# Attention of a prompt: probabilities times values as three products of 64 stationary columns

## The chip, the cores and the metric

The kernel runs on one core of a Trainium2 chip. The metric is the device time of one launch in microseconds, taken as the median of several runs. Of the engines the text speaks of PE (TensorE, with PEld for its weight loads), DVE (VectorE), ACT (ScalarE) and POOL (GpSimd).

## What is computed

The whole kernel is one inference step of a two-layer decoder: a gated DeltaNet layer with its feed-forward part, then a layer of dilated sliding-window attention with its own. The change touches the attention of the prompt (1024 positions), three head groups with a window and a dilation of (128, 1), (512, 4) and (2048, 16), 16 heads of 64 in each group, 4 key/value heads:

```python
def dilated_band_attention(q, win, dil, slope, *, k, v):
    ...
    qr = residues(q).reshape(b, dil, nb, B_BLOCK, nkv, qpk, dh)
    kw = key_windows(k)
    vw = key_windows(v)
    ...
    scores = jnp.einsum('brnqgpd,brnkgd->brngpqk', qr, kw, preferred_element_type=jnp.float32) * (dh ** -0.5) + bias
    scores = jnp.where(valid[:, None, None], scores, -jnp.inf)
    lse = jax.nn.logsumexp(scores, axis=-1)
    probs = jnp.exp(scores - lse[..., None])
    out = jnp.einsum('brngpqk,brnkgd->brnqgpd', probs, vw.astype(jnp.float32))
```

## The kernel before

Matrix products are made of 32-bit numbers split in two: a rounded part in the type that TensorE multiplies at full rate (`F32R`, the names with `hi` or `h`), and the rest, rounded too (`lo` or `l`). A product of two split numbers is usually made as three products (hi x hi, lo x hi, hi x lo) added up in PSUM.

`attn_prompt` goes over 24 units: 4 key/value heads, in each the 3 groups, in each 2 pairs of query heads. A unit has a query projection (`q_proj`: 72 products on L1346, evacuated by ACT and DVE in turn on L1356 and L1357) and an attention (`attend`) over 8 blocks of 128 queries. The projection of unit i + 1 runs beside the attention of unit i. When a key/value head is done, `combine` merges its three groups, beside the second unit of the next head; the last head is merged after the loop.

A block goes through five steps, each a push of a pipeline (`stream`), so that five blocks are under way: `scores` (L1431: four products with the keys' two parts; on DVE bias and row minimum on L1435; on ACT the exponential on L1437), a pause, `flip` (L1450: PE transposes the probabilities of two heads; ACT makes the rounded part `ph` on L1453, DVE the rest `pl` on L1454), a pause, and `outputs`, which the change is in. A block has one or two key blocks of 128 (`span`): 15 key blocks in a unit of the first group, 12 in the second, 8 in the third.

`outputs` before: for each key block the stationary operand is 128 columns wide, the values' rounded part in columns 0 to 63 and their rest in 64 to 127 (`vh[:, kb]`, laid out by `load_kv` on L1382 to L1384). Two products (L1468), with `ph` and with `pl` as the moving operand of 256 columns (2 heads x 128 queries), give all four partial products: PSUM rows 0 to 63 hold (ph + pl) x hi, rows 64 to 127 (ph + pl) x lo. Every second block the bank holds two blocks. ACT then copies rows 64 to 127 to the tile `ot` (L1471), and DVE adds rows 0 to 63 and `ot` into the output tile `og`, once for each of the two heads (L1484). The output tile is in natural order, so the addition's destination is dense in the first group, and has steps of 4 and 16 elements in the other two. There are two PSUM banks for this (tag `o`, L1794), and two each for the projection, the scores and the transposes.

The order of the work has two sources. `merge` (L45) takes turns between generators by the share of work that they report: the projection yields 24 times 1/24 (three products each), the attention 40 times 1/30, so the projection is through when the attention is at three quarters of its 40 pushes, and the last two of the 8 blocks have no projection beside them. Then the framework that builds the program places the instructions of each engine in an order of its own and derives the waits; in the trace the products of one block mostly stand together, but not always. Within an engine the order is fixed, and each instruction waits for its operands and buffers.

```python
        seq = [(k0 + j, x[:, j]) for j in range(nk) for x in parts]
        for j, (kb, x) in enumerate(seq):
            nc.tensor.matmul(po[:, b % 2], vh[:, kb].rearrange("p x d -> p (x d)"), x, start=j == 0, stop=j == len(seq) - 1)
        if b % 2:
            t = bp.tile([64, 2, 2, P], F32, name="ot")
            nc.scalar.activation(t, po[64:], AF.Copy)
```

Other lines that the text names: L1389 and after, transposes of the keys in `load_kv`; L1289, the key/value projection, whose last token tile has 64 tokens, and so 64 stationary columns; L987, products of the DeltaNet layer in plain 32-bit type (`F32`), some of them with 64 stationary columns between the dense products of L764; L1294 and L1645, copies out of PSUM.

Of the kernel before, what the change touches and what calls it, by code (L numbers as in the profile page):

```python
# [13 lines left out]
F32 = mybir.dt.float32  # L14
F32R = mybir.dt.float32r
BF16 = mybir.dt.bfloat16
AF = mybir.ActivationFunctionType
# [5 lines left out]
P = 128  # L23
# [1238 lines left out]
class Attn:  # L1262
# [194 lines left out]
    def outputs(self, i, parts, ap, bp, v, st):  # L1457
        nc = self.nc
        ((kv_, g, pr), qs, (kh, kl, vh), dist, stat), b = i
        k0, nk = self.span(g, b)  # L1460
        if b == 0:
            v["o", kv_, pr, g] = ap.tile([P, SP], F32, tag="og", name="og", bufs=7)
        if b % 2 == 0:
            v["po"] = self.bank("o").rearrange("p (b a q) -> p b a q", b=2, a=2)
        o, po = v["o", kv_, pr, g], v["po"]
        seq = [(k0 + j, x[:, j]) for j in range(nk) for x in parts]
        for j, (kb, x) in enumerate(seq):
            nc.tensor.matmul(po[:, b % 2], vh[:, kb].rearrange("p x d -> p (x d)"), x, start=j == 0, stop=j == len(seq) - 1)  # L1468
        if b % 2:
            t = bp.tile([64, 2, 2, P], F32, name="ot")  # L1470
            nc.scalar.activation(t, po[64:], AF.Copy)  # L1471
            for a in range(2):
                rows = o[64 * a:64 * a + 64]
                if g == 0:
                    dst = rows[:, (b - 1) * P:(b + 1) * P].rearrange("p (b q) -> p b q", b=2)
                elif g == 1:
                    dst = rows.rearrange("p (b q r) -> p r b q", b=2, r=4)[:, b // 2]
                else:
                    dst = rows.rearrange("p (q r) -> p r q", r=16)[:, 2 * (b - 1):2 * (b + 1)]
                x0, x1 = po[:64, :, a], t[:, :, a]  # L1480
                if g == 2:
                    x0, x1 = (x.rearrange("p b (c q) -> p b c q", c=2) for x in (x0, x1))
                    dst = dst.rearrange("p (b c) q -> p b c q", b=2)
                nc.vector.tensor_add(dst, x0, x1)  # L1484
        if b == 7:
            pst = self.bank("tr")
            nc.tensor.transpose(pst[:32, :P], stat.rearrange("p x a b -> p (x a b)"), self.ident)
            row = bp.tile([32, P], F32, name="srow")
            nc.vector.tensor_copy(row, pst[:32, :P])
            for x in range(2):  # L1490
                nc.sync.dma_start(st[kv_, g, 2 * pr:2 * pr + 2, x].rearrange("a (b q) -> a b q", q=P), row[16 * x:16 * x + 16])
# [365 lines left out]
```

## Time and profile before

| | |
|---|---|
| median of 3 runs | 3398.77 us (3397.34 to 3402.65) |
| profiled execution | 3405.86 us |
| its span, first to last instruction | 3404.0 us |
| mean granted clock of TensorE | 0.956 |
| PE busy | 3120.5 us, 92% |
| DVE busy | 2295.2 us, 67% |
| ACT busy | 1559.8 us, 46% |
| POOL busy | 1408.4 us, 41% |

The profile is one execution on the chip. Busy time is the union of an engine's instructions; matmuls are pipelined, so that one is marked longer than it holds up the next. "Idle before" is the time that an engine stood ahead of an instruction, with the instruction that ended the wait behind an arrow. A granted clock of 1.00 is 2.4 GHz, 0.5 is 1.2 GHz. All times of the trace count from the span's start.

### The profile page before, as it was taken

The page shows a single profiled execution, that of the slowest core. Times are in us where ns is not written, and L with a number is a line of the kernel's source. Part 1 is how long each engine was busy: PE and PEld are TensorE (multiplying, and loading weights), DVE is VectorE, ACT ScalarE, POOL GpSimd, SP SyncE. Part 2 cuts the span into 40 slices and gives each one's busy share as a digit, 9 for nine tenths or more (in the row PEclk, how much of TensorE's full clock was granted, in tenths as well). Part 3 has the DMA queues.
Part 4 walks back from the last instruction along what each step waited for, and adds up shares of the span by engine and source line. Part 5 has one row for each costly group of instructions (what it writes and reads, how often), then busy time and mean ns, then how long its engine had stood idle before and what let it go on. Part 6 is the DMA issues. An engine that isn't in the chain of part 4 may idle for free.

```text
span 3404.0 us, 53964 instructions
## 1 busy us (share of the span) xinstructions
PE 3120.5 (92%) x19816; PEld 2841.7 (83%) x19816; DVE 2295.2 (67%) x4757; ACT 1559.8 (46%) x3783; POOL 1408.4 (41%) x1350
## 2 busy tenths in 40 slices
PE   7899999999899999899899899997898999998996
PEld 7888888888799999777688888887586999997774
DVE  5667776624665555688957778787656655556888
ACT  5445544434433333433457676776244333334333
POOL 3333333343454444587631313120123544445877
PEclk9999999999999999999899999998899999999998
DMA  4333333345322221411341111111543222214113
GB/s 135 98 99 98 111 105 98 98 123 184 105 77 77 77 77 64 166 68 61 111 144 44 48 43 53 41 37 35 173 133 102 77 77 77 77 64 163 67 65 111
DMA packets 248837, 311.76 MB, mean 92 GB/s; under 512 B 33058, under 2 KB 204306, under 8 KB 248572
## 3 DMA queue, kind: packets, MB, share of 16 engines
q1 hardware_dynamic: 240572, 276.20, 25.7%
q0 software_dynamic: 7856, 31.56, 2.3%
q8 instruction: 156, 2.56, 0.3%
q14 instruction: 109, 0.89, 0.1%
q10 hardware_dynamic: 144, 0.56, 0.0%
HBM read 227.91 MB, written 80.36 MB: 91 GB/s over the span
## 4 chain that ended last, share of the span: by engine, by line
PE 60%; DVE 16%; POOL 8%; ACT 7%; issue 6%; DMA 4%; SPq 0%; POOLq 0%; DVEq 0%; ACTq 0%
PE mm L355 27%; PE mm L394 6%; PE mm L764 5%; PE mm L567 4%; PE mm L1346 3%; PE B L1054 2%; ACT s L1437 2%; PE mm L1289 1%; DVE yc L811 1%; DVE og L1484 1%; DVE qs L1357 1%; DVE wa L380 1%; PE A L987 1%; DMA vT<-qkv 1%; PE o L1697 1%
## 5 line engine op out<-in xcount | busy, mean ns | idle before, releaser
L394 PE MATMUL mm<-wa,ga 128*128 128x512 f32 x1872 | 476.0, 412 | 62.2 <-DVE wa L380 22.0
L394 PEld LDWEIGHTS mm<-wa,ga 128*128 128x128 f32 x1872 | 367.9, 199 | 164.0 <-DVE wa L380 32.4
L764 PE MATMUL mm<-h_hi,w 128*128 128x352 f32 (+1 forms) x1536 | 444.6, 348 | 10.4 <-ACT xr L801 8.0
L1346 PE MATMUL mm<-h_hi,w 128*128 128x352 f32 (+1 forms) x1152 | 361.9, 348 | 0.1
L764 PEld LDWEIGHTS mm<-h_hi,w 128*128 128x128 f32 x1536 | 282.9, 193 | 22.6 <-ACT xr L801 8.9
L323 POOL TENSOR_TENSOR wide<-wide,v 128x288 f32<-128x288 f32 (+1 forms) x176 | 162.7, 939 | 244.3 <-DVE v L322 244.3
L764 PE MATMUL mm<-h_lo,w 128*128 128x352 f32 (+1 forms) x768 | 259.7, 338 | 0.0
L304 DVE TENSOR_TENSOR s<-w,s 128x512 fp32r<-128x512 f32 x132 | 165.2, 1253 | 128.7 <-ACT s L303 128.5
L303 ACT ACTIVATE s<-t 128x512 fp32r<-128x512 f32 x176 | 111.1, 632 | 287.9 <-PE mm L355 277.5
L294 POOL TENSOR_TENSOR t<-w 128x512 f32<-128x512 f32 x88 | 114.5, 1303 | 298.9 <-issue 138.2
L1346 PEld LDWEIGHTS mm<-h_hi,w 128*128 128x128 f32 x1152 | 216.9, 193 | 2.1 <-DVE qs L1357 0.7
L1437 ACT ACTIVATE s<-s,stat 128x128 f32<-128x128 f32 (+1 forms) x384 | 169.1, 442 | 85.1 <-DVE stat L1435 84.0
L145 POOL TENSOR_TENSOR w<-raw,w 128x1024 fp32r<-128x1024 f32 x38 | 100.6, 2649 | 225.3 <-ACT w L142 128.7
L1346 PE MATMUL mm<-h_lo,w 128*128 128x352 f32 (+1 forms) x576 | 192.5, 334 | 0.0
L567 PE MATMUL mm<-mw_hi,o_hl 128*128 128x512 f32 x544 | 175.6, 400 | 4.0 <-ACT o_hl L555 4.0
L304 DVE TENSOR_TENSOR s<-t,s 128x512 fp32r<-128x512 f32 x176 | 131.6, 749 | 39.7 <-ACT s L303 39.5
L355 PE MATMUL mm<-b0h,s 128*128 128x256 f32 (+1 forms) x704 | 144.6, 293 | 12.3 <-ACT s L303 9.7
L1454 DVE TENSOR_TENSOR pl<-tr,ph 128x256 fp32r<-128x256 f32 (+1 forms) x192 | 104.3, 544 | 71.8 <-ACT ph L1453 70.9
L811 DVE SCALAR_TENSOR_TENSOR yc<-xr,convw,yc 128x1112 f32<-128x1112 f32 x72 | 115.9, 1610 | 54.5 <-ACT yc L809 54.4
L764 PEld LDWEIGHTS mm<-h_lo,w 128*128 128x128 f32 x768 | 149.0, 194 | 1.9 <-issue 0.9
L355 PE MATMUL mm<-b6h,s 128*128 128x256 f32 (+1 forms) x704 | 142.8, 292 | 5.1 <-ACT b6h L190 5.1
L355 PE MATMUL mm<-b1h,s 128*128 128x256 f32 (+1 forms) x704 | 142.9, 291 | 4.9 <-ACT y_mix L570 4.9
(487 smaller groups left out, 9452.4 us busy)
## 6 DMA issues: line engine op xcount, KB each, us to landing
w<-in_ffn_w_in_dram SPq DMA_DIRECT2D x88, 512.0 KB
gd<-wide POOLq DMA_DIRECT2D x22, 1088.0 KB, 5.1
graw<-gd SPq DMA_DIRECT2D x44, 544.0 KB
wraw<-in_ffn_w_out_dram SPq DMA_DIRECT2D x44, 512.0 KB
raw<-in_a_w_in_dram SPq DMA_DIRECT2D x32, 512.0 KB
qkv<-f SPq DMA_DIRECT2D x24, 544.0 KB
xo<-x SPq DMA_DIRECT2D x24, 512.0 KB
raw<-in_b_w_q_dram SPq DMA_DIRECT2D x24, 512.0 KB
```

Of the source, the lines that this page charges most:

```text
L294: op(t, x, y)
L303: nc.scalar.activation(out[j][:, 0], x, AF.Copy)
L304: nc.vector.tensor_sub(out[j][:, 1], x, out[j][:, 0])
L323: nc.gpsimd.tensor_tensor(out, out, v, op=ALU.mult)
L355: nc.tensor.matmul(ps[:, :HC[c][1]], u, v, start=z == 0, stop=z == 11)
L394: nc.tensor.matmul(ps, a, b, start=i == 0, stop=i == len(seq) - 1)
L567: nc.tensor.matmul(ps, a, b[:, k], start=k == 0 and i == 0, stop=k == KD - 1 and i == len(seq) - 1)
L764: nc.tensor.matmul(ps[:, :n], a[:, k, :], b[:, k, n0:n0 + n], start=i_ == 0, stop=i_ == 23)
L811: nc.vector.scalar_tensor_tensor(yc, xr[:, j:j + CW], w(j), yc, op0=ALU.mult, op1=ALU.add)
L1346: nc.tensor.matmul(ps[:, :n], a[:, k, :], b[:, k, n0:n0 + n], start=i == 0, stop=i == 23)
L1437: nc.scalar.activation(s[:, a, :n], s[:, a, :n], AF.Exp, bias=m, scale=-1.0, accum_out=stat[:, 1, a, b:b + 1])
L1454: nc.vector.tensor_sub(pl[:, :nk], pt[:, :nk], ph[:, :nk])
```

## The change

The values' two parts are no longer loaded as one stationary operand of 128 columns, but each as one of 64, and three products instead of two are made for a key block, all into PSUM rows 0 to 63: values' hi x `ph`, hi x `pl`, lo x `ph`. The fourth partial product (lo x `pl`) is left out. Of each pair of blocks ACT then copies the first head from PSUM to the output tile, and DVE the second; the copy to `ot` and the additions are gone.

```diff
         o, po = v["o", kv_, pr, g], v["po"]
-        seq = [(k0 + j, x[:, j]) for j in range(nk) for x in parts]
-        for j, (kb, x) in enumerate(seq):
-            nc.tensor.matmul(po[:, b % 2], vh[:, kb].rearrange("p x d -> p (x d)"), x, start=j == 0, stop=j == len(seq) - 1)
+        ph, pl = parts
+        seq = [(vh[:, k0 + j, u], x[:, j]) for j in range(nk) for u, x in ((0, ph), (0, pl), (1, ph))]
+        for j, (w, x) in enumerate(seq):
+            nc.tensor.matmul(po[:64, b % 2], w, x, start=j == 0, stop=j == len(seq) - 1)
         if b % 2:
-            t = bp.tile([64, 2, 2, P], F32, name="ot")
-            nc.scalar.activation(t, po[64:], AF.Copy)
             for a in range(2):
...
-                x0, x1 = po[:64, :, a], t[:, :, a]
+                x = po[:64, :, a]
                 if g == 2:
-                    x0, x1 = (x.rearrange("p b (c q) -> p b c q", c=2) for x in (x0, x1))
+                    x = x.rearrange("p b (c q) -> p b c q", c=2)
                     dst = dst.rearrange("p (b c) q -> p b c q", b=2)
-                nc.vector.tensor_add(dst, x0, x1)
+                if a:
+                    nc.vector.tensor_copy(dst, x)
+                else:
+                    nc.scalar.activation(dst, x, AF.Copy)
```

## Rows read from the trace of the kernel before

**Rows 1.** The page: busy us, share of the span, instructions.

```profile
PE 3120.5 (92%) x19816; PEld 2841.7 (83%) x19816; DVE 2295.2 (67%) x4757; ACT 1559.8 (46%) x3783; POOL 1408.4 (41%) x1350
```

**Rows 2.** Windows: width, busy PE, PEld, DVE, ACT, POOL (instructions), clock, DMA share, GB/s.

```profile
1816.00:2345.00 529.00, 481.82 (x3212) 452.72 (x3211) 418.54 (x1236) 384.37 (x1090) 113.36 (x72) 0.97 0.15 40
```

**Rows 3.** Groups by line and shape, 1760 to 2372 us: busy us, mean ns, idle before.

```profile
L1484 DVE TENSOR_TENSOR og<-o,ot 64x256 f32<-64x256 f32 x192 | 104.0, 541 | 12.5 <-ACT ot L1471 9.5
...
L1468 PE MATMUL o<-ph,vh 128*128 128x256 f32 x280 | 82.8, 306 | 5.1 <-ACT ph L1453 2.9 <-DVE og L1484 1.8
...
L1471 ACT ACTIVATE ot<-o 64x512 f32<-64x512 f32 x96 | 57.1, 595 | 15.4 <-PE o L1468 13.2
```

**Rows 4.** Timeline of PE: start, duration, line, operation, operands.

```profile
2175.44 0.28 PE L1468 MATMUL o<-ph,vh 128*128 128x256 f32 x1
...
2175.91 0.33 PE L1346 MATMUL mm<-h_hi,w 128*128 128x352 f32 x1
```

**Rows 5.** The sum over five windows with the projection in them.

```profile
sum 95.80, PE 94.19 PEld 92.68 DVE 72.10 ACT 69.57 POOL 11.64; mean PE 18.84 PEld 18.54 DVE 14.42 ACT 13.91 POOL 2.33
```

**Rows 6.** The other five windows of that head: two of them, and their sum.

```profile
2079.00:2122.00 43.00, 35.99 (x218) 29.84 (x216) 38.36 (x97) 27.35 (x70) 21.33 (x16) 1.00 0.25 70
...
2189.00:2193.30 4.30, 1.78 (x11) 1.21 (x10) 3.75 (x10) 4.23 (x12) 1.75 (x1) 1.00 0.01 2
...
sum 60.30, PE 46.85 PEld 38.97 DVE 53.04 ACT 44.19 POOL 26.28; mean PE 9.37 PEld 7.79 DVE 10.61 ACT 8.84 POOL 5.26
```

**Rows 7.** L1468 alone (PE, PEld) in the five windows of rows 5.

```profile
2059.90:2079.00 19.10, 3.20 (x18) 2.90 (x18) 1.00 0.13 32
2122.00:2140.00 18.00, 3.71 (x23) 3.47 (x24) 1.00 0.01 3
2146.00:2165.00 19.00, 3.03 (x18) 2.85 (x18) 1.00 0.24 67
2170.00:2189.00 19.00, 3.34 (x18) 2.89 (x18) 1.00 0.12 32
2193.30:2214.00 20.70, 2.90 (x14) 2.70 (x14) 0.92 0.25 68
```

**Rows 8.** Timeline of PE at the end of the key/value projection's 64-token tile.

```profile
1720.62 0.39 PE L1289 MATMUL mm<-w,h_hi 128*64 128x512 f32 x1
1720.86 1.04 PE L187 MATMUL sm<-ident,xn 128*128 128x128 f32 x8
```

**Rows 9.** Groups by line: copies from PSUM; last, min/median/max of the additions.

```profile
L1645 DVE COPY kt<-tr 128x264 f32<-128x264 f32 x8 | 3.4, 427 | 0.6 <-PE tr L1640 0.6
...
L1356 ACT ACTIVATE qs<-mm 64x288 fp32r<-64x288 f32 x48 | 27.9, 582 | 3.1 <-PE mm L1346 2.5 <-DVE qs L1357 0.6
L1294 ACT ACTIVATE kv_o<-mm 64x256 f32<-64x256 f32 x3 | 0.9, 371 | 2.4 <-PE mm L1289 2.4
...
L1484 DVE TENSOR_TENSOR og<-o,ot x192: 401/599/631, 1778.7 to 2370.2; 64x256 f32<-64x256 f32 x192
```

**Rows 10.** Who waited for whom: total us, times, longest.

```profile
ACT qs L1356 <- DVE qs L1357: 14.5, 29, 1.1
```

**Rows 11.** Timeline of DVE, then of PE, at a unit's end.

```profile
2190.85 1.19 DVE L1484 TENSOR_TENSOR og<-o,ot 64x256 f32<-64x256 f32 x2
...
2192.73 0.30 PE L1431 MATMUL sc<-kh,qs 128*128 128x128 f32 x1 [1.64 <-DVE stat L1435]
```

**Rows 12.** L1484 alone in the windows of rows 6: the long one, and the sum.

```profile
2079.00:2122.00 43.00, 4.13 (x10) 1.00 0.25 70
...
sum 60.30, DVE 8.97; mean DVE 1.79
```

**Rows 13.** Timeline of PE in the recurrent layer.

```profile
107.41 0.32 PE L764 MATMUL mm<-h_lo,w 128*128 128x352 f32 x1
107.57 0.32 PE L764 MATMUL mm<-h_hi,w 128*128 128x352 f32 x1
107.81 0.33 PE L987 MATMUL A<-kT 128*64 128x64 f32 x2
```

## The prediction

> **What bounds the kernel now.** I read the profile's page first: TensorE is marked busy 92% of the span, weight loads 83% [rows 1]. The profiled execution took 3405.86 us, 1.9 us more than its span of 3404.0 and 7.1 us (0.2%) more than the 3398.77 us median of the three runs; I work out a difference on the trace and put it on the median. 0.2% of the median, 6.8 us, is also about what a measurement of this kernel can tell from no change.
>
> The change sits in the prompt's attention, some 610 us from 1760 us on. A table by stretch shows what kind of stage that is: in 529 us of it TensorE is marked busy 482 us, VectorE 419 us, ScalarE 384 us, at a granted clock of 0.97 [rows 2]. The reader is to see three engines near their limits, so shares don't decide and the stage has to be cut finer.
>
> The groups by line give the pieces: two times 280 products of 256 columns on L1468 (the row with `pl` is the twin of the one with `ph`), 96 copies `ot` on ScalarE of 595 ns, and 192 additions `og` on VectorE of 541 ns, 104.0 us in all [rows 3]. The 0.3 us that a product is marked there overlaps with its neighbours; what it takes from the stream is the distance of starts. In a timeline of four products in a row, the first starts at 2175.44 and the next line's product at 2175.91: 0.47 us for four, so **0.12 us each** [rows 4].
>
> I then cut one key/value head (2059.9 to 2216.0 us, the third of four) into ten windows. Five of them, 95.8 us together, are those in which the query projection is interleaved: TensorE is marked busy 94.2 us of them, VectorE only 72.1, ScalarE 69.6 [rows 5]. There TensorE sets the time. The other five, 60.3 us, are the ends of units, where there is no projection left to put between, and a long one in which the previous head is merged: TensorE 46.9, VectorE 53.0, ScalarE 44.2 [rows 6]. In those, VectorE or ScalarE sets the time: in the one at 2189 us TensorE has 1.78 of 4.3 us, ScalarE 4.23.
>
> **What is added: 280 products.** A key block has two products now and three after, so 560 become 840. At 0.12 us, 280 x 0.12 = 33.6 us of TensorE's stream. In the TensorE-bound windows stand 18 + 23 + 18 + 18 + 14 = 91 of this head's 140 products [rows 7], 65%. I take the same share of the whole: 0.65 x 33.6 = **21.8 us exposed**. The other 11.8 us fall where TensorE idles 13.4 us per head (60.3 less 46.9 [rows 6]); I count them at nothing, the cover being VectorE's and ScalarE's queues. If that cover goes, the 11.8 come back, and 33.6 is the upper bound.
>
> A product with 64 stationary columns and 256 moving ones doesn't occur. Below: the same 0.12 us, since it moves the same 256 columns. The nearest rows are the key/value projection's last token tile, also of the rounded 32-bit type by the code (L162, L1289): 64 stationary columns, 512 moving: the last starts at 1720.62, the transposes after it at 1720.86 [rows 8], so 0.24 us for twice the columns, and next to nothing extra on leaving. I take 0.12. The upper bound is the rival of the mode, below.
>
> **What is removed and moved: the copy out.** Per pair of blocks, one `ot` copy (64x512) and two additions go; one ScalarE copy and one VectorE copy, each 64x256, come.
> - VectorE. The nearest copy out of PSUM is 128x264 in 427 ns with a dense output [rows 9]; the additions of 64x256 run from 401 (dense output) to 631 ns (spread), 599 in the middle [rows 9]. A dense addition thus costs what a copy does, and I price the copy like the addition, 541 ns. 96 of 192 go: **-52 us of VectorE's work**. Bounds: 427 gives -63, 631 gives -43.
> - ScalarE. A dense 64x256 copy out of PSUM is 371 ns (three of them). With an output spread by 1, 4 and 16 elements in turn, 64x288 takes 582 ns on average [rows 9]; if the dense third is near 390 (371 for 256 columns, and 32 more), the spread two thirds are near 680. So the new copy is some 380 ns for the undilated third, some 620 for the rest: 32 x 380 + 64 x 620 = 52 us against 96 x 595 = 57. **-5 us**, and in two of three groups ScalarE gets no shorter. Bounds: 371 for all, -21 us; 680 for all, +8.
> - Does VectorE's copy still wait for ScalarE's? It needs no result of it now. But ScalarE's second `qs` copy waits 29 times, 14.5 us, for VectorE's operation on the first, with which it shares only the bank in PSUM [rows 10]. So I expect the two copies of a bank to go one after the other, as now (`og` waited 9.5 us for `ot` [rows 3]). Bounds: 0 and -9.5 us of VectorE idling.
> - ScalarE's copy waits for the block's last product, as `ot` did; behind it in that queue are the exponentials of the next blocks. That product is up to 0.24 us later. No DMA is added or moved; the spare tile `ot` only frees memory.
>
> **What the saving is worth.** VectorE's 52 us count only where it is waited for. At 2189 us this can be seen: TensorE stands 1.64 us until VectorE's `stat`, and shortly before that VectorE ran two `og` of 1.19 us together [rows 11]. One of them goes. In the five windows outside TensorE's, `og` takes 9.0 us of VectorE per head, of it 4.1 in the long one [rows 12]. There VectorE has 38.4 of 43 us and ScalarE 27.4 [rows 6]: the half of 4.1 counts in full, 2.1 us, three times (after the last head it is merged elsewhere): 6.2. In the four short ones ScalarE is as full as VectorE or fuller (4.23 against 3.75 us of 4.3), so of the half of 4.9 I count half, 1.2 us, four times: 4.8. **Together -11 us**; bounds 0 and -18 (4 x 4.5).
>
> **Sum:** +21.8 - 11.0 = +10.8 us. 3398.8 + 11 gives **3410 us**.
>
> **Rivals.**
> 1. The two cancel (no change). If half of the exposed 21.8 us is swallowed at the next unit end, where TensorE waits anyway, 10.9 - 11.0 is nothing: 3399 us. For: each unit has such a wait. Against: VectorE's 72.1 of 95.8 us [rows 5] says that it carries no backlog into it, so the end starts later too.
> 2. Faster: the unit ends are set by work that doesn't hang on the added products (`qs` and key splits already queued), so all of the 21.8 is absorbed, and VectorE's saving counts in full: -18, 3381 us. It decides from the point where more than half of the exposed time is absorbed. For: `og` stands shortly before the awaited `stat` [rows 11]. Against: ScalarE, which hardly gets shorter, is full there.
> 3. Entering and leaving 64 columns costs a drain. In the recurrent layer four products of 64 columns stand between products of 128: the step in is 0.24 us (107.57 to 107.81) where the same product otherwise takes 0.16 (107.41 to 107.57) [rows 13]: 0.08 us, and I take as much for the step out. With at least 192 visits (24 units of 8 blocks) of 0.16 us that is 31 us more: 3410 + 31 = 3441 us. Against: those are plain 32-bit products by the code, and the rounded ones of rows 8 leave without a pause.
>
> The Trainium skill, "TensorEngine Tiling (Array Packing)", section "Key Properties", states that changing the tiling mode drains TensorE, which speaks against this change; by that rule the time is rival 3's. This trace agrees for the plain type and not for the rounded one (0.24 us on leaving), and I go by the latter.
>
> **Chances.** Forecast (over 3406, its own range 3406 to 3425) 0.45; rival 1 0.29; rival 2 0.18; rival 3 0.08. So faster 0.18, same 0.29, slower 0.45 + 0.08 = 0.53. The range reaches down into rival 2, whose lower half it leaves out (0.09), and up to the full 33.6 us less a little relief, 3430, without rival 3 (0.08): 3388 to 3430.
>
> **What would show it.** Right: 840 products on L1469 or so, still 0.12 us apart, no pause around them; windows with the projection longer by some 0.06 us per old product, TensorE as full as before; VectorE's group of copies near 52 us; shorter waits for `stat` and `pl` at unit ends. Wrong: the projection windows unchanged in length (rival 1 or 2); a gap of weight loads before the first or after the last 64-column product (rival 3); ScalarE's copies well over 620 ns, which would turn the unit ends longer; or a changed order of instructions that opens waits in the projection windows.

## The result and the profile after

The changed kernel took 3383.25 us (median of 7 runs, 3378.46 to 3390.45), the kernel before, beside it on the same chip, 3401.23 us (7 runs, 3393.71 to 3406.94). The ratio is **0.9948, interval 0.9932 to 0.9963**: 18 us faster, with an interval of 13 to 23 us. The forecast was 11 us slower, and the range's lower end was 3388 us: forecast and range were both wrong.

The busy line of the page after, which answers to [rows 1]:

```profile
PE 3121.5 (92%) x20096; PEld 2847.5 (84%) x20096; DVE 2252.6 (67%) x4661; ACT 1541.1 (46%) x3783; POOL 1408.5 (42%) x1350
```

TensorE has 280 instructions more and is marked busy 1 us longer; VectorE lost 43 us, ScalarE 19. The groups by line of 1754 to 2360 us, as in [rows 3] (the products and the two copies):

```profile
L1469 PE MATMUL o<-ph,vh 128*64 128x256 f32 x560 | 135.3, 290 | 0.3
...
L1469 PE MATMUL o<-pl,vh 128*64 128x256 f32 x280 | 79.9, 286 | 0.0
...
L1486 ACT ACTIVATE og<-o 64x256 f32<-64x256 f32 x96 | 51.9, 541 | 0.8 <-PE o L1469 0.7
L1484 DVE COPY og<-o 64x256 f32<-64x256 f32 x96 | 51.7, 539 | 9.4 <-ACT og L1486 8.0
```

There are 840 products. (Behind L1468 the changed kernel's lines stand up to two further on.) VectorE's copy takes 539 ns and ScalarE's 541, and VectorE waits 8.0 us for ScalarE's copy of the same bank. A timeline of TensorE, which answers to [rows 4]:

```profile
2176.85 0.32 PE L1346 MATMUL mm<-h_hi,w 128*128 128x352 f32 x1
2177.01 0.28 PE L1469 MATMUL o<-ph,vh 128*64 128x256 f32 x1
2177.13 0.28 PE L1469 MATMUL o<-pl,vh 128*64 128x256 f32 x1
2177.24 0.28 PE L1469 MATMUL o<-ph,vh 128*64 128x256 f32 x1
2177.36 0.32 PE L1346 MATMUL mm<-h_hi,w 128*128 128x352 f32 x1
```

The 64-column products start 0.12 us apart, and nothing is added on entering (0.16 us, the distance that projection products have among themselves) or on leaving (0.12 us).

**Where the time went.** I cut both profiled executions at the first and the last score product (L1431) and at the decode's first product of cache keys. A window from the first to the last score product, before and then after (width, busy time of PE, PEld, DVE, ACT, POOL, granted clock, DMA share, GB/s):

```profile
1759.90:2362.50 602.60, 547.53 (x3668) 516.62 (x3668) 475.89 (x1420) 443.27 (x1264) 125.46 (x78) 0.97 0.15 41
```

```profile
1754.80:2349.30 594.50, 560.08 (x3943) 531.63 (x3943) 432.33 (x1335) 425.97 (x1265) 123.75 (x78) 0.99 0.17 47
```

The attention became 8.1 us shorter with 275 more of TensorE's instructions on record in it. TensorE's time without a mark fell from 55.1 (602.6 - 547.5) to 34.4 us. The granted clock rose from 0.97 to 0.99: the window before has 34.1 us at the lower of the two levels, the window after 13.7, each such stretch behind a pause of TensorE. A part of one of them in the kernel before, and two products in it:

```profile
2195.00:2198.00 3.00, 3.00 (x13) 3.00 (x12) 1.53 (x7) 1.47 (x7) 0.00 (x0) 0.50 0.68 191
```

```profile
2195.41 0.52 PE L1346 MATMUL mm<-h_lo,w 128*128 128x384 f32 x1
2195.73 0.52 PE L1346 MATMUL mm<-h_hi,w 128*128 128x384 f32 x1
```

Products of 384 columns start 0.32 us apart there, and 0.17 us at the upper level (2198.40 and 2198.57). So the clock gives at most half of the 20.4 us, some 10 us, and that is as much as the whole shortening. The decode's first product of cache keys, before and then after (duration min/median/max, first and last start):

```profile
L1660 PE MATMUL s<-kt,qb x160: 279/386/690, 2385.3 to 2472.4; 128*64 128x256 f32 x64, 128*64 128x264 f32 x64, 128*64 128x136 f32 x32
```

```profile
L1662 PE MATMUL s<-kt,qb x160: 279/386/690, 2358.7 to 2443.6; 128*64 128x256 f32 x64, 128*64 128x264 f32 x64, 128*64 128x136 f32 x32
```

From the last score product to it passed 22.8 us before (2385.3 - 2362.5) and 9.4 us after (2358.7 - 2349.3): 13.4 us less. I call this stretch **the gap**. The rest is the start of the attention, 5.1 us earlier with the same instructions ahead of it, so by how much two executions differ, and the part behind the gap, 0.7 us longer: -8.1 - 13.4 - 5.1 + 0.7 = -25.9, the difference of the spans (3404.0 and 3378.1). Half of it thus lies in a stretch of which the prediction doesn't speak. The queue of SP shows what happens there, before and then after (start, time, line, DMA):

```profile
2360.43 1.21 SPq L1491 DMA_DIRECT2D st<-srow  x2
...
2369.25 1.21 SPq L1491 DMA_DIRECT2D st<-srow  x2
2371.83 1.25 SPq L1575 DMA_DIRECT2D kc<-in_cache_k_dram  x2
```

```profile
2332.26 1.27 SPq L1577 DMA_DIRECT2D kc<-in_cache_k_dram  x2
...
2345.61 1.28 SPq L1493 DMA_DIRECT2D st<-srow  x2
...
2357.48 1.27 SPq L1493 DMA_DIRECT2D st<-srow  x2
```

The decode's first cache load, `kc`, was the last in line before, behind the row writes of the last units. After the change it goes ahead of the last two of them, 17 us ahead of the last score product.

### The profile page after: what moved, and what is told of

Its sections match the earlier page's. It is cut to its first block, busy times and chain, and to the rows that moved or that the text cites. A ratio compares the mean times of both kernels' runs of the same rounds, so it can differ in the third digit from the quotient of the medians.

```text
span 3378.1 us, 54405 instructions
## 1 busy us (share of the span) xinstructions
PE 3121.5 (92%) x20096; PEld 2847.5 (84%) x20096; DVE 2252.6 (67%) x4661; ACT 1541.1 (46%) x3783; POOL 1408.5 (42%) x1350
## 3 DMA queue, kind: packets, MB, share of 16 engines
q1 hardware_dynamic: 240572, 276.20, 25.9%
## 4 chain that ended last, share of the span: by engine, by line
PE 63%; DVE 14%; POOL 8%; ACT 6%; issue 6%; DMA 3%; SPq 0%; POOLq 0%; ACTq 0%; DVEq 0%
PE mm L355 27%; PE mm L394 6%; PE mm L764 5%; PE mm L1346 5%; PE mm L567 4%; PE B L1054 2%; PE mm L1289 1%; DVE yc L811 1%; ACT s L1437 1%; PE sc L1431 1%; PE o L1469 1%; DVE wa L380 1%; PE A L987 1%; PE tr L1450 1%; DVE qs L1357 1%
## 5 line engine op out<-in xcount | busy, mean ns | idle before, releaser
L394 PEld LDWEIGHTS mm<-wa,ga 128*128 128x128 f32 x1872 | 364.5, 197 | 167.2 <-DVE wa L380 34.1
L764 PE MATMUL mm<-h_hi,w 128*128 128x352 f32 (+1 forms) x1536 | 440.4, 345 | 10.3 <-ACT xr L801 8.1
L1346 PE MATMUL mm<-h_hi,w 128*128 128x352 f32 (+1 forms) x1152 | 354.4, 342 | 0.0
L764 PEld LDWEIGHTS mm<-h_hi,w 128*128 128x128 f32 x1536 | 280.1, 191 | 22.1 <-ACT xr L801 9.0
L1346 PEld LDWEIGHTS mm<-h_hi,w 128*128 128x128 f32 x1152 | 212.3, 189 | 1.6
L1346 PE MATMUL mm<-h_lo,w 128*128 128x352 f32 (+1 forms) x576 | 189.3, 329 | 0.0
```

The source lines that it names most:

```text
L394: nc.tensor.matmul(ps, a, b, start=i == 0, stop=i == len(seq) - 1)
L764: nc.tensor.matmul(ps[:, :n], a[:, k, :], b[:, k, n0:n0 + n], start=i_ == 0, stop=i_ == 23)
L1346: nc.tensor.matmul(ps[:, :n], a[:, k, :], b[:, k, n0:n0 + n], start=i == 0, stop=i == 23)
```

## The experiments

Ratios are to the kernel before, run beside each kernel on the same chip; 0.001 is 3.4 us.

**Parts of the change, with the loads held in place.** In all kernels said to be pinned, the decode's cache loads are kept behind the last row write on SP, where they stood before:

```diff
-                nc.sync.dma_start(st[kv_, g, 2 * pr:2 * pr + 2, x].rearrange("a (b q) -> a b q", q=P), row[16 * x:16 * x + 16])
+                self.last_st = nc.sync.dma_start(st[kv_, g, 2 * pr:2 * pr + 2, x].rearrange("a (b q) -> a b q", q=P), row[16 * x:16 * x + 16])
...
+            with tc.issue_after(self.last_st.ins):
```

The kernel before with the pin alone:

> The kernel before, with the decode part's cache loads tied on SP's queue behind the last write of the softmax rows (st), where the kernel before has them anyway. Every theory: as the kernel before, within 0.2%, decode's first score product about 23 us after the attention's last one. It is the base for the three runs beside it.

The changed kernel with the pin:

> The changed kernel with the same tie of the cache loads. Theory A (the 18 us come from two places: about 8 from the attention itself and about 12 from cache loads that stand earlier on SP's queue): 12 us slower than the changed kernel, so some 8 us (0.2%) faster than the kernel before, with the gap between the attention's last score product and decode's first one back at 20 us or more. Theory B (all of it comes from the attention, the loads' place is worth nothing): as the changed kernel, 18 us (0.5%) faster than the kernel before.

The products alone (old copy-out):

```diff
-        seq = [(k0 + j, x[:, j]) for j in range(nk) for x in parts]
+        seq = [(k0 + j, x[:, j]) for j in range(nk) for x in (*parts, parts[0])]
```

> The kernel before with the tie, and a third product of 128 columns for each key block (ph a second time, so that the sum is another one); the copy out is the old one. 280 products of 0.12 us alone. By the prediction's exposed share: +22 us on p0 (bounds 12 to 34). By the absorbed view (rival 2): under +5 us.

The copy-out alone (the two old products):

```diff
-            t = bp.tile([64, 2, 2, P], F32, name="ot")
-            nc.scalar.activation(t, po[64:], AF.Copy)
...
-                nc.vector.tensor_add(dst, x0, x1)
+                if a:
+                    nc.vector.tensor_copy(dst, x)
+                else:
+                    nc.scalar.activation(dst, x, AF.Copy)
```

> The kernel before with the tie, its two products of 128 columns, and the new copy out: ScalarE copies the first head, VectorE the second, rows 64 to 127 (values' rest) are left out. The copy's saving alone. By the prediction: -11 us on p0 (bounds 0 to -18). If the saving was mis-sized and the exposed share was right: -30 us or more. If the products were absorbed and the saving right: -8 to -18.

And twice as many products as before, with the old copy-out:

> The kernel before with four products per key block instead of two, 128 stationary columns each (the sum holds the first probabilities three times), copy-out as before; cache loads pinned behind the last row write. 67 us more of TensorE's stream, at 0.12 us each. p2_third_product, with 33.6 us more, was 1.5 to 4.5 us slower only. Theory K (stalls of TensorE in the attention take the first 30 or so us and little more): +20 to +40 us, ratio 1.006 to 1.012. Rival (VectorE and ScalarE set the pace throughout, TensorE has room for all of it): +3 to +10 us, ratio 1.001 to 1.003.

Measured: pin alone 1.0003 (0.9988 to 1.0019); changed and pinned 0.9961 (0.9948 to 0.9974); third product alone 1.0013 (1.0001 to 1.0025); copy-out alone **0.9919** (0.9899 to 0.9939); four products 1.0058 (1.0046 to 1.0070). The window from the first to the last score product, in the order pin alone, third product, fourth product, copy-out alone, changed and pinned:

```profile
1753.50:2352.80 599.30, 544.14 (x3668) 513.05 (x3668) 475.83 (x1420) 442.64 (x1264) 125.63 (x78) 0.98 0.15 41
```

```profile
1758.10:2364.20 606.10, 565.41 (x3943) 538.11 (x3944) 477.81 (x1421) 444.61 (x1265) 123.37 (x78) 0.99 0.15 41
```

```profile
1758.30:2378.10 619.80, 590.72 (x4218) 571.05 (x4219) 477.88 (x1419) 446.08 (x1265) 126.73 (x78) 0.99 0.15 40
```

```profile
1757.30:2333.90 576.60, 536.11 (x3667) 508.19 (x3667) 436.33 (x1332) 422.68 (x1265) 123.33 (x78) 0.99 0.17 45
```

```profile
1754.90:2355.50 600.60, 565.89 (x3943) 537.16 (x3943) 433.15 (x1337) 425.99 (x1265) 123.23 (x78) 0.98 0.16 43
```

Width less PE is TensorE's time without a mark: 55.2, 40.7, 29.1, 40.5 and 34.7 us. With the old copy-out 280 more products add 21.3 us of marked time, and the stretch grows by 6.8 only, since 14.5 us of unmarked time go. In the timings they cost 3 us (1.0013 less 1.0003, at most some 13 by the outer ends, 1.0025 less 0.9988). The next 280 cost 15 (1.0058 less 1.0013): the room was nearly used up. With the new copy-out the first 280 cost 14 us (0.9961 less 0.9919). The copy-out alone saves some 28 us (0.9919 less 1.0003), more than the whole change. The pin also gives most of the gap back: 21.6 us with the pin alone (2374.4 - 2352.8), 17.4 us in the changed and pinned kernel (2372.9 - 2355.5).

The room for the products wasn't in the stretches that TensorE is marked to fill. Two runs of projection products (L1346) in the third head, with the pin alone and then with the third product:

```profile
2146.36:2155.16 8.80, 8.80 (x65) 8.73 (x64) 7.08 (x21) 5.45 (x15) 0.00 (x0) 1.00 0.37 95
2195.47:2203.61 8.14, 8.14 (x59) 8.07 (x59) 5.92 (x22) 5.25 (x19) 0.00 (x0) 1.00 0.38 103
```

```profile
2158.34:2167.49 9.15, 9.15 (x68) 9.07 (x67) 7.20 (x21) 6.37 (x19) 0.00 (x0) 1.00 0.32 90
2206.97:2215.33 8.36, 8.36 (x61) 8.29 (x61) 6.12 (x22) 5.33 (x19) 0.00 (x0) 1.00 0.36 100
```

TensorE is marked busy all the time; three and two products of L1468 are added, and the runs are 0.35 and 0.22 us longer, 0.11 to 0.12 us for each. There the products cost what they were priced at. Here is the whole window, cut into such runs (no break of over 1.1 us between two products of L1346) and the rest, in us:

| | runs | of L1468 in them | rest | TensorE unmarked in the rest | at the lower clock, in both |
|---|---|---|---|---|---|
| pin alone | 440.6 | 353 of 560 | 158.5 | 51.9 | 23.9 |
| third product | 436.0 | 437 of 840 | 169.9 | 33.7 | 10.2 |
| copy-out alone | 439.9 | 356 of 560 | 136.5 | 33.4 | 17.1 |
| changed and pinned | 432.5 | 434 of 840 | 167.9 | 32.3 | 27.3 |

Of the 280 added products only 84 stand in the runs with the old copy-out, and 78 with the new one. The others stand in the rest, where TensorE waits. The third product alone takes those waits from 52 to 34 us, the copy-out alone takes them to 33, and both together leave 32: they draw on the same waits. That is one reason why the products cost 3 us in one kernel and 14 in the other. (The lengths of the runs alone don't show a cost: the framework orders TensorE's other products anew in these kernels, and some 70 of them leave the runs.)

The clock is another. In the kernel before, 0.001 more of an execution's mean granted clock goes with 1.7 to 2.3 us less time (six sets of 16 to 28 executions), and the kernels differ in it by several times that. Means of the executions, against those of the kernel before beside them; the last two columns are an estimate at 2 us for each 0.001:

| kernel | time, us | mean clock | the clock's part | left |
|---|---|---|---|---|
| third product, pinned | +3.9 | +0.0045 | -9 | +13 |
| copy-out alone, pinned | -28.1 | +0.0025 | -5 | -23 |
| changed and pinned | -14.1 | +0.0051 | -10 | -4 |
| changed (second measurement, below) | -18.1 | +0.0056 | -11 | -7 |
| changed, `ot` kept (below) | -11.3 | +0.0055 | -11 | 0 |
| before, one buffer of `ot` (below) | -17.9 | +0.0038 | -8 | -10 |

By this the third product's 3 us are a cost of some 13 us, most of which the clock gives back, and of the changed kernel's 18 us more than half come with the clock. (0.001 of 3400 us is 6.8 us at the other level, so at most 3.4 us of work.) Since the lower stretches stand behind pauses of TensorE, the clock isn't apart from the edits; but no run holds it in place, and how much of each difference is the clock's stays an estimate.

**What the copy-out saves by.** Three theories: the work that goes from the two engines, the order in which they have to read one bank, and how evenly each pair's copies are shared. First both copies on VectorE:

```diff
-                if a:
-                    nc.vector.tensor_copy(dst, x)
-                else:
-                    nc.scalar.activation(dst, x, AF.Copy)
+                nc.vector.tensor_copy(dst, x)
```

> Two products of 128 stationary columns as before, both copies out on VectorE and none on ScalarE; the products' second half (rows 64 to 127 of the bank) isn't added, so the sum lacks the rest of the values; cache loads pinned behind the last row write. Compared with the kernel before, ScalarE loses some 57 us of copies and VectorE keeps its 104 us (192 copies for 192 additions). Theory V (it is VectorE's work that TensorE waits for, and the new copy-out paid by halving it): most of the 28 us of p3_new_copy are lost again, ratio 0.998 to 1.001. Theory C (the chain from the last product of a pair over ScalarE's copy to VectorE's two additions held the bank and both queues; or ScalarE's work counted): ratio 0.991 to 0.995, as p3_new_copy.

Then, by the same edit with the other call, both on ScalarE:

> The same with both copies on ScalarE and none on VectorE. Against the kernel before VectorE loses 104 us, ScalarE gains 2 x 53 - 57 = some 49 us. Theory V: VectorE's relief counts fully, ratio 0.985 to 0.992, at least as fast as p3_new_copy. Theory S (both engines are near their limit, and ScalarE becomes what TensorE waits for): ratio 0.996 to 1.003.

Measured 0.9948 (0.9936 to 0.9961) and 0.9948 (0.9930 to 0.9966): 19 us of the 28 (0.9948 less 1.0003), both times. Neither theory V nor theory S holds; it makes no difference which engine is relieved. Then the old copy-out without the data dependence:

```diff
-                x0, x1 = po[:64, :, a], t[:, :, a]
+                x0, x1 = po[:64, :, a], self.ident[:64, None, :].to_broadcast([64, 2, P])
```

> The kernel before with VectorE's additions reading the identity tile instead of ScalarE's copy ot: the same 96 copies and 192 additions of the same sizes, but an addition no longer needs the copy's result; cache loads pinned behind the last row write. The sum holds a constant in place of the values' second half. Theory C (the chain over the two engines, last product, ScalarE's copy, VectorE's two additions, is what the new copy-out shortened): a good part of the 17 us that both one-engine variants gained, ratio 0.994 to 0.998. Theory W (what counts is work: all three variants with the new copy-out took some 55 us off the two engines together): ratio 0.999 to 1.001.

0.9996 (0.9985 to 1.0007), but it doesn't show what I wanted it to. A timeline of ScalarE and VectorE in it:

```profile
2104.85 0.59 ACT L1471 ACTIVATE ot<-o 64x512 f32<-64x512 f32 x1
...
2105.48 0.42 DVE L1484 TENSOR_TENSOR og<-o,ident 64x256 f32<-64x256 f32 x1 [0.44 <-ACT ot L1471]
```

The addition still waits for a copy whose result it doesn't read. The two share the bank alone. The Trainium skill, "PSUM — Partial Sum Buffer", section "PSUM bank collisions raise a hardware error", says that the compiler's back end orders any two engines that touch one bank in the same 32 partitions, readers too; here one reads rows 64 to 127 and the other rows 0 to 63, and they are ordered all the same (9.6 us in 26 waits). So the bank had to go as well:

```diff
-            nc.scalar.activation(t, po[64:], AF.Copy)
+            nc.scalar.activation(t.rearrange("p b a q -> p (b a) q"), self.ident[:64, None, :].to_broadcast([64, 4, P]), AF.Copy)
```

> As r1_unchained, and ScalarE's copy ot (still 64x512) reads the identity tile instead of the bank in PSUM: the number and sizes of the operations on ScalarE and VectorE stay, but nothing of the copy-out stands between the two engines any more, and VectorE's additions shouldn't show a wait for ot (26 waits, 9.6 us, in r1_unchained although the data were independent). The sum holds a constant in place of the values' second half; cache loads pinned. Theory C (the order of the two engines at one bank is what cost the time): ratio 0.994 to 0.997. Theory W (it is the work of some 55 us that the new copy-out takes off): ratio 0.999 to 1.001.

0.9993 (0.9979 to 1.0006). This doesn't tell the two apart either, for another reason: copies that wait for nothing were all issued early. The group of `ot`, then the windows of the first key/value head and of the other three:

```profile
L1471 ACT ACTIVATE ot<-ident x96: 612/620/656, 1744.7 to 1877.7; 64x512 f32<-64x512 f32 x96
```

```profile
1755.00:1904.60 149.60, 135.22 (x916) 128.80 (x916) 108.53 (x329) 137.26 (x375) 21.04 (x11) 0.97 0.17 45
1904.60:2355.10 450.50, 412.64 (x2752) 385.61 (x2753) 363.22 (x1091) 287.73 (x885) 102.25 (x68) 0.98 0.14 39
```

And the same two windows of the kernel with both copies on VectorE:

```profile
1754.80:1893.70 138.90, 131.23 (x917) 127.00 (x917) 106.67 (x329) 96.65 (x289) 21.51 (x11) 0.99 0.18 49
1893.70:2342.10 448.40, 410.40 (x2752) 383.10 (x2752) 362.62 (x1091) 287.63 (x885) 102.26 (x68) 0.98 0.15 43
```

With `ot` crowded into the first head, that head is 10.7 us longer at 40.6 us more of ScalarE's work, with no order at a bank at all (at most 3 of the 10.7 are the clock's: 10.2 us at the lower level against 3.4); in the other three, where both kernels have the same work, they take nearly the same. So ScalarE's work seems to cost time even where TensorE is marked busy 135 of 150 us; TensorE's order of work is another in this kernel, too, and the two aren't parted. How much of the 19 us the order at the bank adds stays open.

**Sharing.** Both copies of a bank on one engine, in turn from pair to pair: the same work as in the change on each engine, and no order at the bank.

```diff
-                if a:
+                if b // 2 % 2:
                     nc.vector.tensor_copy(dst, x)
```

In the changed kernel, not pinned:

> The changed kernel with both copies of a bank on one engine, ScalarE and VectorE in turn from pair to pair: as much work for each engine as in the changed kernel, and none of its 19 waits (8.0 us) of VectorE's copy for ScalarE's at the same bank. Theory C: 4 to 10 us faster than the changed kernel, ratio to the kernel before 0.990 to 0.993. Theory W, or TensorE setting the pace: as the changed kernel, 0.994 to 0.996.

With the two old products, pinned:

> The two products of 128 stationary columns, both copies of a bank on one engine, ScalarE and VectorE in turn from pair to pair (p3_new_copy with the copies shared out as in s2_engine_by_pair); the sum lacks the rest of the values; cache loads pinned. Theory E (work taken off the two engines counts by a third, 55 us for 17; sharing each pair evenly between them is worth another 11 us; the added products then cost some 14): a saving like that of the two one-engine variants, ratio 0.993 to 0.997. Rival (turn by turn is bad in itself, through the order of work that it makes): ratio 0.998 to 1.002.

Both copies on VectorE, three products, pinned:

> The changed kernel with both copies on VectorE; cache loads pinned. By theory E the saving of 17 us of q1_two_copies_vector less some 14 for the products: ratio 0.997 to 1.001. Rival (the products cost nothing where the copy-out is uneven, as with the old copy-out): ratio 0.994 to 0.996.

And the changed kernel, not pinned, with the engines exchanged (`if not a` for `if a`):

> The changed kernel with the two copies exchanged: VectorE takes the first head, ScalarE the second. The same work on each engine, shared evenly in each pair. By theory E as the changed kernel, ratio 0.993 to 0.996. Rival (the gain hangs on the particular order of work that the changed kernel has): anywhere up to 1.000.

All of the copy-outs together:

| copy-out of a pair | two products | three products |
|---|---|---|
| before's: copy `ot`, two additions | 1.0003 (0.9988 to 1.0019) | 1.0013 (1.0001 to 1.0025) |
| one copy on each engine | 0.9919 (0.9899 to 0.9939) | 0.9961 (0.9948 to 0.9974) |
| both on VectorE | 0.9948 (0.9936 to 0.9961) | 1.0010 (0.9999 to 1.0022) |
| both on ScalarE | 0.9948 (0.9930 to 0.9966) | not run |
| both on one engine, in turn | 0.9946 (0.9928 to 0.9963) | 0.9999 (0.9988 to 1.0010), not pinned |

Every way to copy without the addition takes 58 to 65 us off the two engines together (by the windows, against the pin alone) and saves some 19 us with two products. Sharing each pair evenly saves 9 to 10 more (0.9948 or 0.9946 to 0.9919) and 17 with three (1.0010 to 0.9961). Theory C fell here as the main cause: the variants without order at a bank are the slower ones. In each new copy-out that was run both ways the third product costs 14 to 21 us. With the engines exchanged: **0.9916** (0.9896 to 0.9936), median 3379.37 us, at least as fast as the changed kernel with the same three products; the interval overlaps that of the changed kernel's second measurement, below, by a little. So the gain doesn't hang on one lucky order. TensorE's other products stand in another order in each variant of the copy-out, though, and what that does isn't parted from the sharing.

Why sharing counts is argued, not shown. Of the waits, those of VectorE and of ScalarE that lead the lists, before and then after (total us, times, longest):

```profile
DVE pl L1454 <- ACT ph L1453: 70.9, 74, 1.4
...
ACT s L1437 <- DVE stat L1435: 84.0, 95, 1.8
```

```profile
DVE pl L1454 <- ACT ph L1453: 105.7, 99, 2.0
...
ACT s L1437 <- DVE stat L1435: 90.0, 101, 1.6
```

In many blocks VectorE waits for ScalarE's `ph` and ScalarE for VectorE's `stat`. So the two queues may largely work one after the other, and two copies in a row on one of them (1.1 us) may hold up both. One wait fits this for sharing in turn: with two products, VectorE waits 41.5 us (60 times) for ScalarE's `qs` copies, and 11.6 us (32 times) with one copy on each engine. With both copies on VectorE it is 10.0 us (32 times), so this isn't the whole cause.

**Work that no longer counts.** The values' split moved to GpSimd:

```diff
-        nc.scalar.activation(vh[:, :, 0], t[:, :, 2], AF.Copy)
-        nc.vector.tensor_sub(vh[:, :, 1], t[:, :, 2], vh[:, :, 0])
+        nc.gpsimd.tensor_copy(vh[:, :, 0], t[:, :, 2])
+        nc.gpsimd.tensor_sub(vh[:, :, 1], t[:, :, 2], vh[:, :, 0])
```

> The changed kernel with the splitting of the values (12 copies of 628 ns on ScalarE, 12 subtractions of 693 ns on VectorE) moved to GpSimd, which is busy 122 of 585 us in this stage: VectorE -8.3 us, ScalarE -7.5 us. If work of ScalarE and VectorE still counts by about half, as in the experiments so far: 3 to 8 us faster than the changed kernel, ratio to the kernel before 0.991 to 0.994. If TensorE alone sets the pace now: as the changed kernel, 0.995.

> The changed kernel itself, beside the other two: ratio 0.993 to 0.997, as measured before.

0.9943 (0.9928 to 0.9957) against 0.9942 (0.9928 to 0.9957): nothing. 16 us of work taken off once per group, ahead of need, are worth nothing.

**The place of the cache loads.** A first try in the kernel before, not pinned:

```diff
-                nc.sync.dma_start(st[
+                (nc.gpsimd if kv_ == NKV - 1 and g == 2 else nc.sync).dma_start(st[
```

> The kernel before, unpinned, with the row writes of the last key/value head's last group issued on GpSimd's queue instead of SP's, so that the decode's cache loads no longer stand behind them on SP. Theory A (the place of the cache loads on SP is worth the 12 us by which the gap between the last score product and the decode's first product shrank in the changed kernel's trace): ratio 0.996 to 0.998. Rival (the gap is filled by the last head's merging anyway, or the loads are waited for elsewhere): ratio 0.999 to 1.001.

1.0002 (0.9989 to 1.0015). The loads hardly moved, though the row writes of the last two units no longer stood ahead of them:

```profile
2359.71 0.67 SPq L1514 DMA_DIRECT2D mst<-st  x2
2368.45 1.28 SPq L1575 DMA_DIRECT2D kc<-in_cache_k_dram  x2
```

SP issues nothing for 8 us and then the load. So the row writes weren't what held it, and theory A wasn't tested by this. What the change also does is to give back `ot`, two buffers of 2 KB per partition, which later tiles can take. Two kernels part this from the rest: the changed one with `ot` kept,

```diff
+            t = bp.tile([64, 2, 2, P], F32, name="ot")
+            nc.gpsimd.memset(t[:, 0, 0, :8], 0.0)
```

> The changed kernel with the tile ot allocated as before (two buffers of 64x512) and touched once per pair by a GpSimd write of eight columns, which nothing reads. Theory M (the memory that ot gives back lets the decode's cache tiles start earlier: in the changed kernel's trace kc is issued at 2332.26 us, ahead of the last two row writes, and before behind them): kc is issued behind the last row write again, the gap between the last score product and the decode's first is 15 to 22 us instead of 9, and of the gain some 4 to 6 us are lost: ratio 0.996 to 0.998. Rival (the place of the loads has another reason, or is worth nothing): as the changed kernel, 0.994 to 0.995.

and the kernel before with half of it given back:

```diff
-            t = bp.tile([64, 2, 2, P], F32, name="ot")
+            t = bp.tile([64, 2, 2, P], F32, name="ot", bufs=1)
```

> The kernel before, unpinned, with one buffer for ot instead of two, nothing else. Theory M: the cache loads are issued early as in the changed kernel, the gap between the last score product and the decode's first shrinks from 22 to 8 to 12 us, and the time falls by 4 to 13 us, ratio 0.996 to 0.999 (a second copy ot then waits for the additions of the first, which stand a pair earlier: nothing). Rival: 0.999 to 1.001.

With `ot` kept 0.9967 (0.9956 to 0.9977); **with one buffer less, and nothing else changed, 0.9946 (0.9926 to 0.9966)**, as much as the whole change. SP's queue with `ot` kept (its lines stand four further on than before), then with one buffer:

```profile
2349.44 1.21 SPq L1495 DMA_DIRECT2D st<-srow  x2
2351.99 1.26 SPq L1579 DMA_DIRECT2D kc<-in_cache_k_dram  x2
```

```profile
2345.29 1.27 SPq L1575 DMA_DIRECT2D kc<-in_cache_k_dram  x2
...
2359.27 1.28 SPq L1491 DMA_DIRECT2D st<-srow  x2
...
2367.16 1.31 SPq L1491 DMA_DIRECT2D st<-srow  x2
```

Kept, the load is behind the last row write again; freed, it is ahead of the last two. In the kernel with one buffer the attention and the decode's first product:

```profile
1756.40:2361.30 604.90, 551.39 (x3668) 520.47 (x3668) 475.38 (x1421) 443.53 (x1264) 124.96 (x78) 0.96 0.16 45
```

```profile
L1660 PE MATMUL s<-kt,qb x160: 279/386/689, 2371.7 to 2455.9; 128*64 128x256 f32 x64, 128*64 128x264 f32 x64, 128*64 128x136 f32 x32
```

The gap is 10.4 us (2371.7 - 2361.3) against 22.8 before, and the attention is no shorter (604.9 against 602.6). TensorE's and ScalarE's instructions in the attention stand in the same order as before. Theory M holds, and more than I expected of it: the trace shows 12 us, the timing 18 (12 to 25).

## Why the prediction was wrong, point by point

- **"Together -11 us; bounds 0 and -18"** is the step that failed by most: the copy-out alone is worth some 28 us, or some 23 without what is put down to the clock. The prices were right (VectorE's group went from 104.0 [rows 3] to 51.7 us, ScalarE's from 57.1 to 51.9), and the copies of one bank do go one after the other. It also counts where I looked for it: between the pin alone and the copy-out alone the runs of projection products stay as long (440.6 and 439.9 us), and the rest goes from 158.5 to 136.5. Wrong was how much it counts there: I took half of the time of `og` in those windows, with 18 us as the bound, and the rest became 22 us shorter in the traces. Why it gains more than VectorE's own time isn't shown.
- **"the spare tile `ot` only frees memory"** put at nothing what lay in the next stage. Freed memory is what let the cache loads start early: the gap is 9.4 us in the changed kernel, and 17.4 and 21.8 with the loads held back (pinned, and `ot` kept, 2365.6 - 2343.8). It is worth 18 us in the timing alone, and 4 to 6 us on top of the rest. I looked for DMAs that the change adds or moves and found none in its lines; the one that it moved belongs to the next stage.
- **The clock had no term**, though [rows 7] show 0.92 in one window behind a unit's end, where TensorE had waited. It is put at nothing without a reason, and by the estimate above it goes with 10 to 11 us of the changed kernel's gain.
- **"0.65 x 33.6 = 21.8 us exposed"** came out about right in size (14 to 21 us with the new copy-outs) and not in its way. The share was taken from the old products, of which 63% stand in the runs (353 of 560); of the added ones 30% do (84 of 280). That the others count "at nothing" holds only as long as TensorE waits in the rest anyway. The prediction names this ("If that cover goes, the 11.8 come back") but not that its own saving takes the cover: 3 us for the products and 28 for the copy-out make 14 together, not 25. "There TensorE sets the time" stands where I could look: in two runs that are marked full each product cost its 0.11 to 0.12 us.
- The sum: with the loads pinned, -28 + 14 gives -14 us, measured 0.9961 less 1.0003, where I had +10.8, so most of the error is here. The freed memory takes the changed kernel from 0.9961 to 0.9948 and 0.9942, 4 to 6 us more. With memory alone at -18 and the rest alone at -11 (`ot` kept), the two overlap by some 10 us, within wide intervals. By the estimate it is the clock's parts that don't add up (8 and 11 us apart, 11 together); why they don't stays open.
- 0.12 us per product was right. Rival 3 fell: no drain on entering or leaving. The rule of the Trainium skill, "TensorEngine Tiling (Array Packing)", "Key Properties", costs nothing here that a row shows, as [rows 8] had it, and unlike the plain type in [rows 13].
- Rival 2 gave 3381 us, close to what was measured, by another way: it had the products absorbed, which holds only with the old copy-out and partly by the clock, and knew of neither the freed memory nor the evenness. Rival 1's time was wrong; its mechanism, added time swallowed where TensorE waits anyway, is seen in part with the third product alone.

## What to carry to other kernels

An addition that is to hide in an engine's waits and a saving that shortens the same waits can't be priced one by one: price them together, or try each alone, since each changes what the other costs. Set the granted clock of both kernels beside their times before a cost is put down to work. Where two engines copy out of PSUM and also wait for each other, try giving each of them a copy of every pair rather than whole pairs in turn. And of a tile that a change removes, ask what the next stage loads into its memory: one buffer less, by itself, was worth here as much as the whole edit.

## What the hardware showed that I had not expected

In a row of score products with 128 moving columns, each costs about as much of TensorE's stream as one with 256. The timeline of score products after:

```profile
2050.55 0.22 PE L1431 MATMUL sc<-kh,qs 128*128 128x128 f32 x1
2050.61 0.28 PE L1431 MATMUL sc<-kl,qs 128*128 128x128 f32 x1
2050.72 0.27 PE L1431 MATMUL sc<-kh,qs 128*128 128x128 f32 x1
2050.83 0.28 PE L1431 MATMUL sc<-kl,qs 128*128 128x128 f32 x1
...
2055.74 0.28 PE L1431 MATMUL sc<-kh,qs 128*128 128x256 f32 x1
2055.86 0.28 PE L1431 MATMUL sc<-kl,qs 128*128 128x256 f32 x1
2055.98 0.28 PE L1431 MATMUL sc<-kh,qs 128*128 128x256 f32 x1
```

The starts are 0.12 us apart for 256 columns and 0.11 us for 128, except behind the first of the row, which follows a product of 256 columns: 0.06 us. So the moving columns alone don't set the 0.11 us. The weight loads of the next three start as far apart (2050.56, 2050.66, 2050.78); whether they set it isn't shown. By this, products cut in two by heads should be nearly twice as dear in a row (an estimate); my rule that the cost goes with the moving columns holds from 256 to 512 [rows 8], and not below in such a row.
